# Even layer of a two-layer encoder trunk: the plan that orders its instructions knows three forms of TensorE products, and its ranks are searched anew

## The chip, the cores and the metric

The kernel runs on one core of a Trainium2 chip. The metric is device time in microseconds, the median of several executions. The engines named here are TensorE (PE, with its weight loads PEld), VectorE (DVE), ScalarE (ACT), GpSimd (POOL) and SyncE (SP), which issues the DMAs. Each engine works through its own instructions in the order in which the program gives them, and semaphores hold an instruction back until its inputs are there.

## What is computed

The trunk has two residual layers over 512 tokens of width 1024. Each has a mixer, a layer norm, a convolutional FFN and a second norm. The change touches the mixer of layer 0 alone:

```python
def attn_s5_mixer(x, w_in, sink, a_re, a_im, log_dt, b_re, b_im, c_re, c_im, d_skip, w_glu, w_out):
    z = x @ w_in
    q, k, v, u = jnp.split(z, [ATTN_WIDTH, ATTN_WIDTH + KV_WIDTH, ATTN_WIDTH + 2 * KV_WIDTH], axis=-1)
    y_attn = windowed_gqa(q, k, v, sink)          # 8 heads of 64, window of 128 keys each way
    y_s5 = s5_mixer(u, a_re, a_im, log_dt, b_re, b_im, c_re, c_im, d_skip, w_glu)
    y = jnp.concatenate([y_attn, y_s5], axis=-1)
    return y @ w_out
```

The attention has eight heads and a softmax over up to 384 keys for each block of 128 queries. The S5 part is a bidirectional diagonal complex state-space layer over 32 groups of 16 channels with 64 states each, followed by a GELU and a gate (GLU).

## The kernel before

Every large product is done in three parts of reduced precision: each operand is split into a high part and a low part of type fp32r (`xh`, `xl`, `wh`, `wl`), and `mm3` (line 533) multiplies high by high, high by low and low by high into one PSUM bank. A unit of weights is 512 KB: SP loads it into a staging tile `st` (two of them), ACT casts it to `wh`, and DVE, or POOL for the later units, subtracts to get `wl` (`load_unit`, line 494). `proj_T` (line 539) makes one projection of 128 columns from one unit: 24 products of 512 columns.

The even layer is not issued as it is written. Its methods record steps in a `Plan` (line 200): units 0 to 3 give the S5 inputs (`e_u`), units 4 and 5 give k and v (`e_kv`), units 6 to 9 give q (`e_q`); then come the scores and softmax of each head (`att_scores`), the transposed probabilities times v (`att_out`), and for the S5 part a set-up of narrow steps of 32 columns on DVE (`s_small`, `s_phase`), and for each of four blocks of eight groups the input products (`s_in`), the rotation and the scan on DVE (`s_rot`), tables (`s_out_tables`), the short-range kernel (`s_lags`, with a round trip through DRAM) and the output products (`s_y`, with a second round trip). Three of the four token tiles of the first half of the output projection (`out0` to `out2`) are recorded too; they fill PE where it would wait. Behind the plan GLU (`s_glu`, line 1207) and the rest of the output projection follow, issued in the order in which they are written.

Products come in three shapes of stationary tile. The projections, and the transposes (a product with the identity, `ident`), load a full tile of 128 by 128. The S5 products and the probabilities times v are plain fp32 and use tiles of 128 by 64, one half of the array's columns; each of them stands as two records in the trace. The scores contract over 64 rows: tiles of 64 by 128.

`Plan.order` (line 324) is a list scheduler. It keeps a clock for each engine, knows a cost for every step (`cost`, line 288) and a hop time between engines (`HOP`). Among the steps that can start within 0.06 us of the earliest it takes the one of highest rank:

```python
            s.prio = t + max((steps[u].prio + self.hop(s, steps[u]) for u in s.users), default=0.0)
            s.rank = s.prio + BIAS.get(s.part, 0.0)
```

The rank is the longest weighted path to the end (weights of the engines in `WEIGHT`) plus a number for the step's part, from the table `BIAS`. All engines' instructions, SP's DMAs among them, are issued in the order that results. All instructions of the plan carry line 436, in which they are issued.

Of the kernel before, what the change touches and what calls it, by code (L numbers as in the profile page):

```python
# [45 lines left out]
for _h in range(2, 8):  # L46
    ODD_UNITS += [(c, _h) for c in "qko"]
    if _h % 2 == 1 and _h < 7:
# [11 lines left out]
BIAS = {"act0": 6194, "act1": 110, "act2": 2791, "act3": -1269, "att0": 3695, "att1": 1849, "att2": 2975,  # L60
# [14 lines left out]

WEIGHT = dict(tensor=1.0844148001145095, vector=3.5473736157196103, scalar=0.1530721205110878, gpsimd=0.02, sync=0.09043312895279432)
# [111 lines left out]
class Step:  # L188
    __slots__ = ("eng", "name", "args", "kw", "deps", "users", "cost", "size", "table", "port", "first", "claims", "roots", "prio", "rank", "part", "end", "left", "at")
# [10 lines left out]
class Plan:  # L200
# [4 lines left out]
    HOP = dict(tensor=0.26, vector=0.16, scalar=0.2, gpsimd=0.16, sync=0.1)  # L205
# [30 lines left out]
    def record(self, eng, name, args, kw):  # L236
# [31 lines left out]
        s.port = self.port(s)  # L268
        s.users, s.end, s.at = [], None, None
# [18 lines left out]
    def cost(s):  # L288
        free = lambda v: math.prod(v.shape[1:])
        kw = s.kw  # L290
        if s.eng == "tensor":
            if s.name == "transpose":
                return 2 * free(s.args[1]) / 2400.0
            n = free(kw["rhs"])
            if kw["rhs"].f32r:
                return n / 2400.0 + 0.0133
            n = 4 * max(n, kw["lhsT"].shape[1]) / 2400.0

            return 0.04 if s.args[0].shape[0] == 64 and s.args[0].box[0][0] == 64 else n
# [5 lines left out]
        if s.eng == "scalar":  # L305
            if s.name == "activation":
                s.table = {AF.Exp: 0, AF.Gelu_apprx_tanh: 1, AF.Tanh: 1}.get(kw["func"])
            return 0.085 + 0.00083 * n + 0.09 * sum(not isinstance(kw.get(k, 0.0), float) for k in ("scale", "bias")) + 0.09 * ("accum_out" in kw)
# [15 lines left out]
    def order(self):  # L324
# [8 lines left out]
        table = None  # L333
# [1434 lines left out]
```

## Time and profile before

| | |
|---|---|
| median of 3 runs | 1302.25 us (1301.97 to 1305.85) |
| profiled execution | 1303.45 us, of which the span of instructions is 1301.3 us |
| TensorE busy | 1264.2 us (97%), 6938 products |
| VectorE busy | 717.4 us (55%) |
| ScalarE busy | 547.7 us (42%) |
| GpSimd busy | 138.6 us (11%) |
| planned part | from the start to 230.0 us, when the first product of GLU (line 535) stands on PE |

A busy share says how long an engine had something in work, not how fast it went: records of PE overlap, and their distance from start to start is what one costs. A stretch of the table by window gives the busy time of each engine in it, so that one sees which engine is full there. The chain of waits goes back from the last instruction to what released it, and shows long pieces of one engine where nothing else is waited for.

### The profile page before, as it was taken

How to read it: one execution, taken by the hardware profiler on the slowest of the kernel's cores; microseconds unless marked ns; L12 is line 12 of the kernel's file. 1: busy time of each engine (PE TensorE's matmuls, PEld its weight loads, DVE VectorE, ACT ScalarE, POOL GpSimd, SP SyncE). 2: the span in 40 equal slices, each digit the busy share in tenths (PEclk: the TensorE clock that was granted, in tenths of full speed). 3: DMA queues.
4: the chain of work that ended last, by engine and by line, in shares of the span. 5: the costliest groups of instructions: out<-in, count | busy, mean ns of one | idle time of the engine just before them, and what ended most of it. 6: DMA issues, size and time to landing. Idle time of an engine off the chain costs nothing.

```text
span 1301.3 us, 17757 instructions
## 1 busy us (share of the span) xinstructions
PE 1264.2 (97%) x6938; PEld 1054.9 (81%) x6938; DVE 717.4 (55%) x1402; ACT 547.7 (42%) x919; POOL 138.6 (11%) x139
## 2 busy tenths in 40 slices
PE   3999999999999999999999999999999999999997
PEld 2787777788888888888889898988888888888886
DVE  9887675576442354433674646374865432544415
ACT  4457576344332143332346646472453321433301
POOL 2100322000000000000004444420000000000000
PEclk9999999999999999999999999999999999999999
DMA  5542323534332243323123223223343322433301
GB/s 178 164 127 55 97 90 98 194 98 136 107 93 89 60 140 99 96 93 105 34 91 105 81 82 97 82 65 116 128 144 101 96 87 75 129 97 98 97 33 64
DMA packets 54627, 130.86 MB, mean 101 GB/s; under 512 B 13616, under 2 KB 22144, under 8 KB 53904
## 3 DMA queue, kind: packets, MB, share of 16 engines
q1 hardware_dynamic: 54544, 129.73, 32.3%
q8 instruction: 54, 0.88, 0.3%
q14 instruction: 29, 0.24, 0.1%
HBM read 124.99 MB, written 4.72 MB: 100 GB/s over the span
## 4 chain that ended last, share of the span: by engine, by line
PE 88%; DVE 7%; ACT 2%; issue 1%; DMA 1%; POOL 0%; DVEq 0%; POOLq 0%; ACTq 0%
PE b L559 20%; PE b L536 17%; PE b L535 17%; PE b L537 17%; PE b L436 12%; PE b L1540 1%; PE b L1542 1%; DMA st<-w_dram 1%; DVE x L601 1%; DVE x L579 1%; DVE wl L519 1%; DVE C L436 0%; DVE t L436 0%; ACT wh L518 0%; PE b L1572 0%
## 5 line engine op out<-in xcount | busy, mean ns | idle before, releaser
L536 PE MATMUL b<-xl,wh 128*128 128x512 f32 (+1 forms) x944 | 357.1, 379 | 1.7 <-DVE xl L616 1.7
L535 PE MATMUL b<-xh,wh 128*128 128x512 f32 (+1 forms) x944 | 357.5, 380 | 1.0 <-ACT xh L615 1.0
L537 PE MATMUL b<-xh,wl 128*128 128x512 f32 (+1 forms) x944 | 356.8, 378 | 0.0
L518 ACT CAST wh<-st 128x1024 fp32r<-128x1024 f32 x175 | 183.5, 1051 | 398.2 <-DMA st<-w_dram 144.6
L519 DVE TENSOR_TENSOR wl<-st,wh 128x1024 fp32r<-128x1024 f32 x153 | 186.9, 1224 | 290.4 <-ACT wh L518 286.6
L536 PEld LDWEIGHTS b<-xl,wh 128*128 128x128 f32 x944 | 177.6, 188 | 35.0 <-DVE xl L616 2.4
L535 PEld LDWEIGHTS b<-xh,wh 128*128 128x128 f32 x944 | 177.1, 188 | 34.4 <-ACT xh L615 1.9
L537 PEld LDWEIGHTS b<-xh,wl 128*128 128x128 f32 x944 | 177.6, 188 | 33.2
L559 PE MATMUL b<-wh,hh 128*128 128x512 f32 x352 | 109.2, 389 | 0.0
L559 PE MATMUL b<-wh,hl 128*128 128x512 f32 x352 | 109.2, 389 | 0.0
L559 PE MATMUL b<-wl,hh 128*128 128x512 f32 x352 | 109.1, 389 | 0.0
L598 POOL TENSOR_TENSOR lnrs<-lnsq,mhalf 128x1 f32<-128x1 f32 x16 | 10.5, 657 | 822.2 <-DVE lnsq L597 822.2
L559 PEld LDWEIGHTS b<-wh,hl 128*128 128x128 f32 x352 | 66.1, 188 | 13.7
L559 PEld LDWEIGHTS b<-wl,hh 128*128 128x128 f32 x352 | 66.1, 188 | 13.7
L559 PEld LDWEIGHTS b<-wh,hh 128*128 128x128 f32 x352 | 66.0, 188 | 13.7
L722 DVE TENSOR_TENSOR c<-c,b 128x512 f32<-128x512 f32 x44 | 30.2, 687 | 64.6 <-PE b L537 61.0
L721 ACT ACTIVATE c<-c 128x512 f32<-128x512 f32 x44 | 27.8, 632 | 80.8 <-DVE c L720 80.8
L519 POOL TENSOR_TENSOR wl<-st,wh 128x1024 fp32r<-128x1024 f32 x22 | 52.5, 2390 | 55.6 <-ACT wh L518 55.6
L579 DVE SCALAR_TENSOR_TENSOR x<-x,b 128x512 f32<-128x512 f32 x48 | 31.3, 684 | 43.9 <-PE b L559 40.5
L436 PE MATMUL b<-xh,wh 128*128 128x512 f32 x80 | 33.7, 423 | 11.1 <-ACT wh L436 10.7
L595 ACT ACTIVATE lnjk<-x,lnmu 128x1024 f32<-128x1024 f32 x16 | 18.4, 1152 | 51.4 <-DVE lnmu L594 51.4
L436 PE MATMUL b<-xh,wl 128*128 128x512 f32 x80 | 33.0, 415 | 6.1 <-DVE wl L436 6.1
(332 smaller groups left out, 1924.3 us busy)
## 6 DMA issues: line engine op xcount, KB each, us to landing
st<-w_dram SPq DMA_DIRECT2D x192, 512.0 KB, 3.6
tb<-s5bT_dram SPq DMA_DIRECT2D x16, 256.0 KB, 3.2
lngb<-ln_dram SPq DMA_DIRECT2D x4, 1024.0 KB, 4.8
nb<-DN SPq DMA_DIRECT2D x16, 256.0 KB, 3.6
t<-xT_dram SPq DMA_DIRECT2D x8, 256.0 KB, 7.2
Tj<-DK SPq DMA_DIRECT2D x32, 64.0 KB, 2.3
x<-x_dram SPq DMA_DIRECT2D x1, 2048.0 KB
out_dram<-x SPq DMA_DIRECT2D x8, 256.0 KB, 2.0
```

The source lines that it names most:

```text
L436: getattr(getattr(nc, s.eng), s.name)(*real(s.args), **real(s.kw))
L518: nc.scalar.copy(out=h, in_=x)
L519: eng.tensor_tensor(out=l, in0=x, in1=h.bitcast(F32), op=ALU.subtract)
L535: mm(ps, lhsT=lh, rhs=rh, start=first, stop=False)
L536: mm(ps, lhsT=lh, rhs=rl, start=False, stop=False)
L537: mm(ps, lhsT=ll, rhs=rh, start=False, stop=last)
L559: mm(acc[h], lhsT=hx[:, tok], rhs=wx[:, 512 * h:512 * h + 512], start=a, stop=b)
L579: self.nc.vector.scalar_tensor_tensor(out=xr, in0=xr, scalar=scale, in1=acc[h], op0=ALU.mult, op1=ALU.add, **kw)
L595: nc.scalar.activation(out=jk, in_=x, func=AF.Square, bias=mu, accum_out=sq)
L601: v.scalar_tensor_tensor(out=x[:, c], in0=y[:, c], scalar=rs, in1=b[:, c], op0=ALU.mult, op1=ALU.add)
L721: nc.scalar.activation(out=c, in_=c, func=AF.Gelu_apprx_tanh)
L722: nc.vector.tensor_tensor(out=c, in0=c, in1=pg, op=ALU.mult)
```

## The change

The tables of numbers are replaced, and the planner's rules are changed. It now gives each product on TensorE a form: T for a transpose, R for a product of fp32r (projections and scores alike), F for plain fp32. When a step of PE is taken whose form is another than the last one's, its start is put later by a time from the table `TURN`; and among the candidates a step that keeps the form gets a bonus, `WEIGHT["form"]`, of 20892 on its rank, against biases of up to some 35000. Several costs are set anew (transposes, fp32r and fp32 products, ScalarE's steps with strided input), and one hop. Line numbers in the planned part move by ten (436 becomes 446). Nothing else is changed: the steps, the engines that do them and the buffers are the same.

```diff
-BIAS = {"act0": 6194, "act1": 110, "act2": 2791, "act3": -1269, "att0": 3695, "att1": 1849, "att2": 2975,
+BIAS = {"act0": -2767, "act1": -12777, "act2": -151, "act3": 6961, "att0": 15813, "att1": -1391, "att2": 21019,
...
-WEIGHT = dict(tensor=1.0844148001145095, vector=3.5473736157196103, scalar=0.1530721205110878, gpsimd=0.02, sync=0.09043312895279432)
+WEIGHT = dict(tensor=0.049344435550977735, vector=0.09687933056372891, scalar=858.7347894980174, gpsimd=0.08499304979878007, sync=115.14517424905796, form=20892.369629590066)
...
-    HOP = dict(tensor=0.26, vector=0.16, scalar=0.2, gpsimd=0.16, sync=0.1)
+    HOP = dict(tensor=0.22, vector=0.16, scalar=0.2, gpsimd=0.16, sync=0.1)
+
+    TURN = {"FR": 0.22, "FT": 0.18, "RF": 0.15, "RT": 0.05, "TF": 0.145, "TR": 0.105}
...
+        s.form = None
+        if eng == "tensor":
+            s.form = "T" if name == "transpose" else "R" if kw["rhs"].f32r else "F"
...
             if s.name == "transpose":
-                return 2 * free(s.args[1]) / 2400.0
+                return 0.118
             n = free(kw["rhs"])
             if kw["rhs"].f32r:
-                return n / 2400.0 + 0.0133
-            n = 4 * max(n, kw["lhsT"].shape[1]) / 2400.0
-
-            return 0.04 if s.args[0].shape[0] == 64 and s.args[0].box[0][0] == 64 else n
+                return n / 2400.0 + 0.02
+            return (0.18 if s.args[0].shape[0] == 64 else 0.213) * max(n, kw["lhsT"].shape[1]) / 128
...
-            return 0.085 + 0.00083 * n + 0.09 * sum(not isinstance(kw.get(k, 0.0), float) for k in ("scale", "bias")) + 0.09 * ("accum_out" in kw)
+            if kw["in_"].root.kind not in BANKS and kw["in_"].ap.ap[-1][0] > 1:
+                return 0.06 + 0.00183 * n
+            return 0.1 + 0.00083 * n + 0.09 * sum(not isinstance(kw.get(k, 0.0), float) for k in ("scale", "bias")) + 0.09 * ("accum_out" in kw)
...
-            start, i, take = max(best, key=lambda b: (steps[b[1]].rank, -b[1]))
+            stay = lambda s: WEIGHT["form"] if s.form is not None and s.form == form else 0.0
+            start, i, take = max(best, key=lambda b: (steps[b[1]].rank + stay(steps[b[1]]), -b[1]))
             s = steps[i]
+            if s.form is not None:
+                start = max(start, clock["tensor"] + self.TURN.get(str(form) + s.form, 0.0))
+                form = s.form
```

What this does to the order is seen at three places. In each row stands the line, the operation, the tile written, the tiles read and the shape of the result.

On TensorE, in the middle of the plan (before: a piece of the fourth q projection, `xh` and `xl` times `wh` and `wl`, about 163 us into the span; `ident,s` and `ident,zx` are transposes of probabilities and of S5 tables, `pT,t` probabilities times v), there stands before:

```order
L436 MATMUL b_1690<-xh_82,wl_984 128x512
L436 MATMUL b_1880<-ident_72,s_1749 128x128 x3
L436 MATMUL b_1690<-xh_82,wh_937 128x512
L436 MATMUL b_1690<-xl_83,wh_937 128x512
L436 MATMUL b_1891<-pT_1872,t_892 64x128 x2
L436 MATMUL b_1690<-xh_82,wl_984 128x512
L436 MATMUL b_1901<-ident_72,zx_1709 128x128
L436 MATMUL b_1891<-pT_1893,t_892 64x128 x3
L436 MATMUL b_1901<-ident_72,zx_1709 128x128 x3
L436 MATMUL b_1690<-xh_82,wh_937 128x512
```

On TensorE after, where the probabilities of the same head are at work (`t,t` are scores of the next one):

```order
L446 MATMUL b_1740<-ident_72,s_1422 128x128 x3
L446 MATMUL b_1751<-ident_72,zx_1432 128x128 x4
L446 MATMUL b_1762<-pT_1726,t_648 64x128 x2
L446 MATMUL b_1771<-t_496,t_1133 128x384
L446 MATMUL b_1771<-t_505,t_1133 128x384
L446 MATMUL b_1771<-t_496,t_1142 128x384
L446 MATMUL b_1777<-t_496,t_1133 128x256
L446 MATMUL b_1777<-t_505,t_1133 128x256
L446 MATMUL b_1777<-t_496,t_1142 128x256
L446 MATMUL b_1787<-ident_72,s_1502 128x128 x3
L446 MATMUL b_1791<-ident_72,zx_1769 128x128 x4
```

The wide products of the projection have gone from between the others to a row of their own, and transposes of both kinds stand together.

On VectorE, around its first low part of x (`xl`), with steps of the S5 set-up (`T`, `th`, `al`, `ns`, `ea`, `eb`, `ec`), before, some 80 rows into its order:

```order
L436 TENSOR_TENSOR th_277<-ee_235,ed_248 128x32
L436 TENSOR_TENSOR T_97<-t_53_239,t_54_242 128x64
L436 TENSOR_TENSOR al_281<-fh_269,ed_248 128x32
L436 TENSOR_TENSOR t_53_239<-T_97 128x128
L436 TENSOR_TENSOR t_54_242<-T_97 128x128
L436 TENSOR_SCALAR ns_286<-pv_73 128x8
L436 TENSOR_TENSOR T_97<-t_53_239,t_54_242 128x128
L436 TENSOR_TENSOR xl_83<-t_111,xh_82 128x512
```

On VectorE after, at the head of its order:

```order
L446 TENSOR_TENSOR xl_83<-t_100,xh_82 128x512
L446 TENSOR_TENSOR wl_150<-st_102,wh_146 128x1024
L446 TENSOR_SCALAR ea_157<-KS_113 128x32
L446 TENSOR_SCALAR eb_160<-ea_157 128x32
L446 TENSOR_SCALAR eb_160<-eb_160 128x32
L446 SCALAR_TENSOR_TENSOR ec_164<-eb_160,ea_157 128x32
L446 TENSOR_SCALAR ee_166<-eb_160 128x32
L446 TENSOR_TENSOR wl_168<-st_109,wh_153 128x1024
```

The low parts have moved ahead of the set-up, whose input `KS` also comes later: SP loads it first before, and after x's first two pieces, two weight units and a bias tile now.

On VectorE after, at the low part of weight unit 5 (`wl_523`, the v projection; `C` are S5 tables, `t_499` and `t_505` k):

```order
L446 TENSOR_TENSOR C_444<-bc_138,b_406 128x512
L446 TENSOR_TENSOR ea_468<-fa_488 128x32
L446 TENSOR_TENSOR t_499<-b_415,t_490 64x512
L446 TENSOR_TENSOR t_505<-b_415,t_496 64x512
L446 CAST t_499<-t_499 64x512
L446 CAST t_505<-t_505 64x512
L446 TENSOR_TENSOR eb_472<-fb_485 128x32
L446 SCALAR_TENSOR_TENSOR p_89_519<-fa_488,fb_485 128x32
L446 TENSOR_TENSOR p_89_519<-ea_468,eb_472 128x32
L446 TENSOR_TENSOR wl_523<-st_326,wh_429 128x1024
```

On TensorE after, the products that read it:

```order
L446 MATMUL b_299<-xh_82,wh_280 128x512
L446 MATMUL b_299<-xl_83,wh_280 128x512
L446 MATMUL b_299<-xh_82,wl_301 128x512
L446 MATMUL b_529<-ident_72,zx_512 128x128 x4
L446 MATMUL b_474<-xh_82,wl_523 128x512
L446 MATMUL b_474<-xh_82,wh_429 128x512
```

Ahead of the four transposes here stand 122 wide products and nothing else on PE; before, half-width products came in after 91 wide ones and eight transposes.

## Rows read from the trace of the kernel before

**Rows 1.** The page, busy time: engine, us, share of span, instructions.

```profile
PE 1264.2 (97%) x6938; PEld 1054.9 (81%) x6938; DVE 717.4 (55%) x1402; ACT 547.7 (42%) x919; POOL 138.6 (11%) x139
```

**Rows 2.** By window: length, busy PE, PEld, DVE, ACT, POOL; granted clock, DMA, GB/s.

```profile
0.00:28.00 28.00, 8.22 (x18) 5.31 (x19) 24.89 (x110) 12.62 (x21) 9.05 (x16) 1.00 0.64 207
28.00:47.30 19.30, 18.86 (x83) 14.72 (x82) 19.17 (x80) 6.63 (x12) 0.00 (x0) 1.00 0.44 133
47.30:103.60 56.30, 55.29 (x567) 45.72 (x566) 48.82 (x106) 29.80 (x49) 8.00 (x15) 1.00 0.45 132
103.60:138.00 34.40, 32.07 (x273) 24.24 (x273) 26.00 (x63) 23.62 (x54) 4.63 (x13) 0.95 0.23 58
138.00:174.00 36.00, 35.88 (x319) 26.52 (x317) 23.97 (x57) 25.25 (x55) 10.57 (x17) 1.00 0.30 89
174.00:199.00 25.00, 25.00 (x265) 20.54 (x265) 16.12 (x50) 19.76 (x46) 6.26 (x10) 1.00 0.31 93
199.00:212.40 13.40, 13.28 (x71) 9.12 (x70) 13.36 (x18) 8.41 (x19) 6.72 (x3) 1.00 0.44 126
212.40:230.00 17.60, 17.60 (x158) 14.37 (x157) 5.39 (x7) 11.79 (x17) 0.00 (x0) 1.00 0.29 74
sum 230.00, PE 206.20 PEld 160.54 DVE 177.73 ACT 137.89 POOL 45.24; mean PE 25.77 PEld 20.07 DVE 22.22 ACT 17.24 POOL 5.66
```

**Rows 3.** Chain of waits: start us, us, what; first wide product of GLU last.

```profile
170.72 40.19 PE b L436 x349
...
230.13 0.23 PE b L535
```

**Rows 4.** Timeline of PE: start us, us, line, out<-in, stationary tile, moving tile, records.

```profile
162.65 0.39 PE L436 MATMUL b<-xh,wl 128*128 128x512 f32 x1
162.88 0.49 PE L436 MATMUL b<-ident,s 128*128 128x128 f32 x3
163.12 0.48 PE L436 MATMUL b<-xh,wh 128*128 128x512 f32 x1
163.44 0.40 PE L436 MATMUL b<-xl,wh 128*128 128x512 f32 x1
163.77 0.65 PE L436 MATMUL b<-pT,t 128*64 128x128 f32 x4
164.35 0.50 PE L436 MATMUL b<-xh,wl 128*128 128x512 f32 x1
164.69 0.27 PE L436 MATMUL b<-ident,zx 128*128 128x128 f32 x1
164.89 0.87 PE L436 MATMUL b<-pT,t 128*64 128x128 f32 x6
165.69 0.55 PE L436 MATMUL b<-ident,zx 128*128 128x128 f32 x3
165.99 0.48 PE L436 MATMUL b<-xh,wh 128*128 128x512 f32 x1
```

**Rows 5.** Timeline of PE, early: in brackets the idle time before and its end.

```profile
19.01 0.80 PE L436 MATMUL b<-xh,wl 128*128 128x512 f32 x1 [5.91 <-DVE wl L436]
...
47.00 0.39 PE L436 MATMUL b<-xl,wh 128*128 128x512 f32 x1
47.34 0.44 PE L436 MATMUL b<-C,B 128*64 128x128 f32 x4
47.71 0.50 PE L436 MATMUL b<-xh,wl 128*128 128x512 f32 x1
48.04 0.40 PE L436 MATMUL b<-xh,wh 128*128 128x512 f32 x1
```

**Rows 6.** Timelines of ACT (the last high part of x) and DVE, early.

```profile
18.04 0.60 ACT L436 CAST xh<-t 128x512 fp32r<-128x512 f32 x1
...
23.57 1.22 DVE L436 TENSOR_TENSOR wl<-st,wh 128x1024 fp32r<-128x1024 f32 x1
24.71 3.67 DVE L436 TENSOR_TENSOR C<-bc,b 128x512 f32<-128x512 f32 x6
```

More of the change, by code (lines that the diff above doesn't have):

```diff
@@ L188 @@
 class Step:
-    __slots__ = ("eng", "name", "args", "kw", "deps", "users", "cost", "size", "table", "port", "first", "claims", "roots", "prio", "rank", "part", "end", "left", "at")
+    __slots__ = ("eng", "name", "args", "kw", "deps", "users", "cost", "size", "table", "port", "form", "first", "claims", "roots", "prio", "rank", "part", "end", "left", "at")
 class PlanEngine:
@@ L332, in order @@
         warm, window, busy = False, 0, 0.0
-        table = None
+        table = form = None
         slots, nxt = {}, {}
```

29 rows, old and new, of the table BIAS are left out of this document.

## Prediction, made before the changed kernel was run

> **What bounds the kernel now.** I read the page first: TensorE (PE) is busy for 97% of the span, VectorE (DVE) for 55% [rows 1]. The change touches only the planned even layer, so the next view is the table by stretch of its first 230 us [rows 2]. Columns two and four carry the argument. From 28 us on PE is busy in nearly every microsecond, while DVE is busy for 19.17 of 19.30 us, then 48.82 of 56.30, and later for 16.12 of 25.00: it is the full engine first and has room later. In the chain of waits the long pieces are TensorE's own: one of 349 products takes 40.19 us with no wait inside [rows 3]. So in the planned stage a microsecond saved on PE counts, as long as DVE delivers.
>
> PE's busy time is no measure of its work, since records overlap; the timeline with its start times is [rows 4]. In an unbroken row a wide product (f32r, 512 columns) takes 0.23 us [rows 3]. Three transposes set between two of them cost only themselves: from 162.65 to 163.44 pass 0.79 us, which is two wide products and 0.33, or 0.11 a transpose. The half-width fp32 records `pT,t` are dearer. Four of them pass in 0.58 us (163.77 to 164.35), six in 0.80 (164.89 to 165.69): 0.11 a record, and 0.14 on top. The wide product before the four takes 0.33 instead of 0.23, the one behind them 0.34. That is 0.35 us for one excursion from the full array (128*128 in the rows) to half of it (128*64) and back: 0.175 a change. Over the whole piece from 163.44 to 165.99 the parts (two wide products, ten records, four transposes) make 2.00 of 2.55 us; the rest over four changes is 0.14 each. At 47.00 to 48.04 [rows 5] the wide product before the four `C,B` records takes 0.34, the one behind them 0.33, and the four nothing on top: 0.21 us for two changes, 0.105 each. So the ends are 0.105 and 0.175; I take 0.15, since most changes that go are around `pT`, `U` and score products, as in the first place.
>
> **The change, part by part.**
>
> *Fewer changes of shape on TensorE.* The instructions are the same in number and kind (592 fp32, 408 f32r, 148 transposes); only their order differs. I counted in both orders where the shape of the stationary tile changes (full 128*128; half width 128*64; the score products, 64*128): 173 times before, 69 after, 104 fewer. At 0.15 us this is **-15.6 us**, between -10.9 (0.105) and -18.2 (0.175), all on the engine that sets the stage's pace. The planner itself counts differently: forms F, R and T, with score products among R and transposes apart; in its count 191 turns become 76, 115 fewer.
>
> The Trainium skill ("TensorEngine Tiling (Array Packing)", Key Properties) says that changing the tiling mode, not just the tile, drains the engine. The rows bear it out: transposes among wide products are free, half-width ones are not. By that rule 104 counts and not 115, which at 0.15 would be 17.3 us.
>
> *An earlier start.* Before, DVE works through the S5 set-up first; PE waits for the low part of the first weights until 19.01 us [rows 5]. After, the low parts `xl` and `wl` stand at the head of DVE's order, and PE's order opens with 122 wide products in a row. How far it gets is set by DVE. The last low part of x needs the last high part: 18.04 + 0.60 = 18.6 us before [rows 6], and after too, since the same transfers stand ahead of it in SP's queue. DVE has done 7.3 us of work by then (four `xl`, at 0.6 as any step of 512 columns, two `wl` at 1.14, both [rows 6], and 15 narrow steps of the set-up, some 2.6). What must be done up to `wl` of weight unit 5 (the v projection): the 24.89 us that DVE did in the first 28 us [rows 2], plus three `xl` (1.8), four `wl` at 1.14 (4.6), four copies of k at 0.6 (2.4) and about 1.1 of small steps: 34.8 us. So this `wl` is ready at 18.6 + 0.6 + (34.8 - 7.3) = 46.7 us. PE waits for it with 122 wide products and 4 transposes done; before, at 47.34, it had done 91 and 8 [rows 5]. Lead: 31 x 0.23 - 4 x 0.11 = 6.7, and 0.6 of time: **-7.3 us**. If DVE reaches it 7 us later, for instance because s5s now lands behind x0, w0, bias and w1 and the set-up waits for it, the lead is nothing; if it comes when the wide products are there, it is about 9.
>
> *Where TensorE alone would end.* Before, PE needs 182.7 us from 47.3 to the end of the plan at 230.0. Less 6.7 and 15.6 this is 160.4, from 46.7: 207.1 us.
>
> *What DVE then allows.* DVE's own work is the same, but less of it is done when PE is further. Of its 177.73 us [rows 2], 34.8 are done at 46.7 us and 2.7 (four steps of 512 columns, as `xl`) lie behind the last scan block (rot3: `rb`, `S`); 140.2 remain. Behind rot3 PE has its tail: before, 17.60 us from 212.40 to 230.00 [rows 2]; after, 27 instead of 36 wide products stand there, so 15.6. With DVE never waiting: 46.7 + 140.2 + 15.6 = 202.5. DVE's best long stretches are 99% (28.00:47.30) and 87% (47.30:103.60). Midway, 93%, gives 150.8 and an end at 213.1. That is later than PE's own 207.1, so DVE's pace is the likelier limit: **+6.0 us** against TensorE alone. The ends are 0 and 16.3 (87%: 223.4).
>
> *The new rules of the planner* (costs, hop, turn times) cost nothing on the chip: they act through the order only. SP's order moves too: s5s later, `bias` between the two DK writes of lags 2 and 3 (SP waits there until the four score tiles of a head are read). Their consumers, y2 and y3, stand over 15 us of PE work later, which hides this; without that cover each costs a few microseconds, and it is inside the ends above.
>
> Behind the plan the order is written by hand and unchanged: GLU and output projection move with the end of the plan. The last S5 block goes through DRAM once more before GLU, with 27 wide products and pv7 behind it on PE; nine fewer than before, which leaves that round trip less cover but, by my sum, enough.
>
> Sum against the profiled execution, 1303.45 us (median of the three runs 1302.25, 1.2 less): -15.6 - 7.3 + 6.0 = -16.9 (end of the plan at 213.1 instead of 230.0): **1286.5, rounded 1286**.
>
> **The rivals.**
>
> (a) *TensorE alone sets the end.* DVE keeps over 97%, and waits vanish on both: end 202 to 207, time 1276 to 1281. For it: DVE's 99% early, when its inputs lay ready. Against it: DVE waits in order for scores that PE makes, and PE for DVE.
>
> (b) *DVE at 87%*, its pace in 47 to 104 us before: end 223.4, -6.6 us, 1297. For it: the same mix of steps, in-order waits. Against it: it was then fed by a PE that lost time on changes.
>
> (c) *The changes were hidden anyway*, so that the grouping buys nothing: then only the lead of 7.3 is left, 1296; with a slow DVE as well, no change. Against it: [rows 4] show the loss between products that wait for nothing.
>
> (d) *Slower: DVE's set-up comes too late and DVE is fed as before.* From 47.3 to 212.4 it was busy for 128.3 of 165.1 us, 78%. At that pace 140.2 us take 180, the plan ends at 242.7 and the time is 1316. It decides from 83.6% down: (230.0 - 46.7 - 15.6) = 167.7 us are there for 140.2. Against it: in these stretches PE was full (25.00 of 25.00), so DVE's idleness followed from PE's.
>
> **How the numbers follow.** Forecast (DVE between 90 and 96%, 1281 to 1291): 0.50. (a) 0.20. (b), with times from 1291 to 1298: 0.12. (c) 0.05 at 1296, and a further 0.06 with a slow DVE, within 0.3%. (d) 0.07. A measurement of this kernel can tell about 0.3% (3.9 us) from no change; so faster 0.50 + 0.20 + 0.12 + 0.05 = 0.87, same 0.06, slower 0.07. The range must leave out no more than 0.2: from 1276 (a TensorE without any wait) to 1298 it leaves out some 0.05 below and 0.13 above.
>
> **What would show it.** In the trace after, starts on PE: an early stretch of 122 wide products up to about 46 us with a wait for `wl` in it; far fewer places with 128*64 rows between 128*128 rows, each still dearer by 0.1 to 0.17 us; GLU's first product at 207 to 218 us; DVE busy for over 90% between 47 us and the last scan. I am wrong if PE shows more idle time than some 10 us after 47 us, if a change of shape costs nothing when no wait is near, or if GLU starts with a wait for the last S5 block.

## The result

The changed kernel takes 1283.97 us (median of four runs, 1282.96 to 1285.5), the kernel before 1302.67 beside it: a ratio of 0.9853, 95% interval 0.9833 to 0.9872, so faster by 1.5%. Forecast were 1286 us, range 1276 to 1298. The profiled run took 1284.29 us. Its page, busy time as in [rows 1]:

```profile
PE 1239.7 (97%) x6938; PEld 1044.2 (81%) x6938; DVE 715.7 (56%) x1402; ACT 547.1 (43%) x919; POOL 135.8 (11%) x139
```

The share of TensorE says nothing: 97% before and after. The table by stretch, to be held against [rows 2], is cut at four places of the prediction: x's last low part ready, `wl` of unit 5 ready, the end of the last scan block, GLU's first product.

```profile
0.00:17.40 17.40, 8.95 (x30) 6.42 (x31) 10.49 (x24) 8.32 (x11) 6.86 (x15) 1.00 0.93 296
17.40:42.60 25.20, 22.59 (x98) 17.47 (x96) 23.55 (x108) 14.43 (x25) 0.61 (x5) 1.00 0.44 140
42.60:193.90 151.30, 137.11 (x1470) 115.17 (x1471) 137.17 (x352) 104.81 (x217) 35.40 (x53) 0.97 0.39 113
193.90:209.90 16.00, 12.75 (x148) 10.47 (x146) 4.38 (x6) 9.93 (x15) 0.00 (x0) 1.00 0.13 35
```

Two things are to be seen. The plan ends at 209.9 us instead of 230.1 [rows 3], 20.2 earlier (the span is 19.1 shorter; the 1.1 us lie between 610 and 1035 us, in code that no part of the change touches). And from 42.6 us on it is VectorE (third pair) that is as full as TensorE: 137.17 of 151.30 us, against 128.3 of 165.1 before (the prediction's sum from [rows 2]). TensorE, which stood still for 3.2 us behind 47 us before, now waits for 17.3 there, in 23 waits. The table of waits names the largest (engine, tile and line, for whom: us in all, times, longest):

```profile
PE b L446 <- ACT pT L446: 7.1, 8, 2.2
PE b L446 <- ACT KS L446: 2.2, 3, 1.0
PE b L446 <- DVE m L446: 2.0, 1, 2.0
```

The start of TensorE, as [rows 5]: 122 wide products and four transposes have started by 41.3 us, where before 92 and 8 had by 47.34 (the count of 91 made ahead of the run is one short). Then comes the forecast wait for `wl`, of 1.03 us.

```profile
39.64 0.39 PE L446 MATMUL b<-xh,wl 128*128 128x512 f32 x1
40.93 0.66 PE L446 MATMUL b<-ident,zx 128*128 128x128 f32 x4 [0.91 <-ACT zx L446]
42.62 0.50 PE L446 MATMUL b<-xh,wl 128*128 128x512 f32 x1 [1.03 <-DVE wl L446]
```

TensorE was also slower at the start of the kernel before. Up to 28.2 us its wide products stand 0.43 us apart, as they do in stretches with a granted clock of 0.50 (0.427 us in e2 below), and 0.23 us from there on:

```profile
27.34 0.63 PE L436 MATMUL b<-xl,wh 128*128 128x512 f32 x1
27.76 0.60 PE L436 MATMUL b<-xh,wl 128*128 128x512 f32 x1
28.44 0.40 PE L436 MATMUL b<-xh,wl 128*128 128x512 f32 x1
28.67 0.39 PE L436 MATMUL b<-xh,wh 128*128 128x512 f32 x1
```

In the changed kernel they stand 0.23 us apart from 11.3 us on. The trace's record of the granted clock begins only at these points, 28.2 and 11.1 us, and the tables print 1.00 for what lies ahead of them.

GLU's first product follows the plan's last two (a row that starts at 209.45) without a wait, at 209.90.

**What the prediction had not seen** stands in the rows of half-width products. Their outputs go to partitions 0 to 63 or to 64 to 127, that is, their stationary tiles stand on one half of the array's columns or on the other. Before, at 192.54 us, four records of `So,C` (two products of one half) take 0.28 or 0.24 us:

```profile
192.54 0.45 PE L436 MATMUL b<-So,C 128*64 128x64 f32 x4
192.82 0.28 PE L436 MATMUL b<-U,T 128*64 128x64 f32 x2
192.94 0.40 PE L436 MATMUL b<-So,C 128*64 128x64 f32 x4
193.18 0.28 PE L436 MATMUL b<-U,T 128*64 128x64 f32 x2
```

In the changed kernel the same products take turns between the halves, and eight records pass in the same 0.24 us (183.39 to 183.63), four of `U,T` in 0.11 where before there were two:

```profile
183.39 0.40 PE L446 MATMUL b<-So,C 128*64 128x64 f32 x8
183.63 0.29 PE L446 MATMUL b<-U,T 128*64 128x64 f32 x4
183.74 0.40 PE L446 MATMUL b<-So,C 128*64 128x64 f32 x8
183.98 0.29 PE L446 MATMUL b<-U,T 128*64 128x64 f32 x4
```

A 64-column fp32 product thus costs 0.117 us behind one on its own half, and 0.058 behind one on the other half: the two run at the same time. The Trainium skill says so ("TensorEngine Tiling (Array Packing)", Key Properties: "Tiles operate independently: Different tiles can execute LdWeights and Matmul in parallel"); the rows agree. The prediction drew on the sentence that stands above it, on the drain, and not on this one. It is the half that counts and not the PSUM bank that they write: on the same half, products into different banks stand 0.116 us apart (median of 144 in the kernel before), and on different halves products into the same bank 0.058 (216 in e12 below). In the plan's order two half-width products in a row stood on different halves 132 times of 512 before, and 383 times of 565 after.

**An account of TensorE.** I took the start times of all 1148 products of the plan, in both traces. A stretch of one shape is charged what its products take in an unbroken row (wide 0.227, half-width as above); what is on top of that up to 0.3 us is put down to the change of shape behind it, and more to a wait; stretches that touch half clock stand apart. Behind 28 us, from before to after: wide products and transposes 57.5 to 47.7 us (the lead: they are done earlier), half-width products 74.7 to 60.1, changes of shape 23.4 to 10.5, waits 2.8 to 15.4, half clock 2.2 to 7.9. That is -9.8 - 14.6 - 12.9 + 12.6 + 5.7 = -19.0 of the 20.1 us. (The last row of wide products, 34 before and 27 after, is not in the account; it is 1.6 us more of the lead.) Three gains, of which one was not forecast, and two losses, of which the forecast knew one in another form.

### The profile page after: what moved, and what is told of

Read it like the earlier page. It is cut to its first block, busy times and chain, and to the rows that moved or that the text cites. A ratio compares the mean times of both kernels' runs of the same rounds, so it can differ in the third digit from the quotient of the medians.

```text
span 1282.2 us, 17748 instructions
## 1 busy us (share of the span) xinstructions
PE 1239.7 (97%) x6938; PEld 1044.2 (81%) x6938; DVE 715.7 (56%) x1402; ACT 547.1 (43%) x919; POOL 135.8 (11%) x139
## 4 chain that ended last, share of the span: by engine, by line
PE 82%; DVE 9%; ACT 3%; DMA 2%; issue 2%; POOL 1%; SPq 0%; DVEq 0%; POOLq 0%; ACTq 0%
PE b L569 21%; PE b L546 18%; PE b L545 18%; PE b L547 18%; PE b L446 5%; DMA st<-w_dram 2%; PE b L1550 1%; PE b L1552 1%; DVE t L446 1%; DVE x L611 1%; DVE x L589 1%; DVE C L446 1%; DVE wl L529 1%; SPq L446 0%; DVE c L446 0%
## 5 line engine op out<-in xcount | busy, mean ns | idle before, releaser
L545 PE MATMUL b<-xh,wh 128*128 128x512 f32 (+1 forms) x944 | 357.7, 380 | 1.0 <-ACT xh L625 1.0
L545 PEld LDWEIGHTS b<-xh,wh 128*128 128x128 f32 x944 | 177.1, 188 | 34.4 <-ACT xh L625 1.9
L608 POOL TENSOR_TENSOR lnrs<-lnsq,mhalf 128x1 f32<-128x1 f32 x16 | 10.5, 657 | 840.5 <-DVE lnsq L607 840.5
L569 PEld LDWEIGHTS b<-wh,hl 128*128 128x128 f32 x352 | 66.1, 188 | 13.7
L569 PEld LDWEIGHTS b<-wl,hh 128*128 128x128 f32 x352 | 66.1, 188 | 13.7
L569 PEld LDWEIGHTS b<-wh,hh 128*128 128x128 f32 x352 | 66.0, 188 | 13.6
L545 PE MATMUL b<-wh,xh 128*128 128x256 f32 (+1 forms) x128 | 37.0, 289 | 0.3 <-ACT xh L625 0.3
```

Source lines behind the costliest of these rows:

```text
L545: mm(ps, lhsT=lh, rhs=rh, start=first, stop=False)
L569: mm(acc[h], lhsT=hx[:, tok], rhs=wx[:, 512 * h:512 * h + 512], start=a, stop=b)
```

## Experiments

All plans have the same 1148 products. "Turns" are pairs of half-width products in a row that stand on different halves. "Waits" is the sum of TensorE's table of waits from 47 us to the plan's end; "half clock" is the time between 12 and 238 us in which the granted clock was 0.5, summed from a table by 2 us. The slow start is not in it, since the record of the clock begins behind it: at 28 to 31 us in the kernel before, e1, e4, e5 and e12, at 11 to 16 us in the others.

| kernel | changes of shape | turns | waits us | half clock us | last product of the plan at | time us | ratio to before, 95% |
|---|---|---|---|---|---|---|---|
| before | 173 | 132 of 512 | 3.2 | 3.4 | 229.7 | 1302.7 | |
| changed | 69 | 383 of 565 | 17.3 | 10.2 | 209.7 | 1284.0 | 0.9853 (0.9833 to 0.9872) |
| e1 regroup | 95 | 149 of 551 | 5.4 | 3.4 | 216.8 | 1289.8 | 0.9878 (0.9856 to 0.9900) |
| e2 split | 173 | 363 of 524 | 10.1 | 27.3 | 226.3 | 1299.2 | 0.9954 (0.9935 to 0.9973) |
| e3 no bonus | 144 | 388 of 525 | 21.4 | 20.5 | 233.6 | 1319.2 | 1.0108 (1.0084 to 1.0132) |
| e5 bonus alone | 94 | 125 of 552 | 15.3 | 20.4 | 237.9 | 1314.1 | 1.0070 (1.0048 to 1.0092) |
| e4 late start | 69 | 383 of 565 | 22.6 | 13.6 | 227.6 | 1302.4 | 0.9985 (0.9969 to 1.0001) |
| e6 early start | 167 | 135 of 515 | 19.0 | 20.5 | 237.5 | 1312.8 | 1.0078 (1.0055 to 1.0101) |
| e7 VectorE relieved | 69 | 383 of 565 | 11.6 | 6.8 | 201.6 | 1276.3 | 0.9795 (0.9773 to 0.9817) |
| e8 TensorE relieved | 69 | 383 of 565 | 22.8 | 30.7 | 213.7 | 1286.6 | 0.9873 (0.9851 to 0.9895) |
| e9 queues | 69 | 383 of 565 | 15.0 | 10.2 | 208.4 | 1280.6 | 0.9828 (0.9808 to 0.9848) |
| e10 search | 82 | 287 of 556 | 16.5 | 27.3 | 214.7 | 1288.6 | 0.9886 (0.9864 to 0.9907) |
| e11 search with lock | 77 | 274 of 557 | 13.7 | 6.8 | 205.7 | 1278.7 | 0.9808 (0.9782 to 0.9835) |
| e12 sides | 95 | 436 of 551 | 7.7 | 6.8 | 211.7 | 1284.6 | 0.9858 (0.9828 to 0.9889) |

Where only the order is other, the kernel has this edit and a list of step numbers:

```diff
-        done = self.order()
+        self.order()
+        done = [self.steps[i] for i in ORDER]
```

### What a change of shape costs, and that it counts

**e1.** The order of before, on TensorE alone with stretches exchanged. For instance (TensorE, at 47 us in [rows 5]; out<-in, columns):

```diff
 MATMUL b<-xl,wh 128x512
-MATMUL b<-C,B 64x128 x2
-MATMUL b<-xh,wl 128x512
-MATMUL b<-xh,wh 128x512
-MATMUL b<-C,B 64x128 x6
-MATMUL b<-xl,wh 128x512
...
 MATMUL b<-xl,wh 128x512
+MATMUL b<-C,B 64x128 x16
```

> The kernel before, with its own ranks, its own start and its own order on every engine but TensorE; there, neighbouring stretches of products are exchanged (none over 8 us, and only where the trace of before shows that the inputs of what comes earlier were there and that the reader of what comes later was not yet waiting), so that the tile shape changes 95 times instead of 173. Theory 1 (each change costs TensorE some 0.15 us, and TensorE's time counts): 78 x 0.15 = 11.7 us less, 1291; 1295 if a third of it goes into waits of its own. Theory 2 (the grouping buys nothing, the gain of the changed kernel is its earlier start): 1302, no change.

1289.77 us, 15.0 less than before beside it (1304.74). The plan's last product starts 12.9 us earlier, which is 0.165 a change for 78 changes, while TensorE's waits grew by 2.2 us only. Its largest waits, before and in e1:

```profile
PE b L436 <- ACT s L436: 1.5, 1, 1.5
PE b L541 <- ACT So L541: 1.8, 2, 1.0
```

So the grouping pays by itself, with before's start and ranks: theory 1. In the account of e1 the places of change fall from 23.4 to 10.1 us, and the turns hardly move (half-width products 74.7 to 73.4). The median of what a change adds in the kernel before is 0.15 us behind full-array stretches, 0.14 behind half-width ones, 0.19 behind score products (57, 78 and 33 stretches).

**e2.** The changed kernel, cut up again on TensorE until the shape changes 173 times:

```diff
-MATMUL b<-U,t 64x64 x2
-MATMUL b<-ident,s 128x128 x4
+MATMUL b<-U,t 64x64
+MATMUL b<-ident,s 128x128
+MATMUL b<-U,t 64x64
+MATMUL b<-ident,s 128x128 x3
```

> The changed kernel, with its start and the order of every other engine as they are; on TensorE, behind 28 us, stretches of two shapes that stand side by side are cut into two pieces each and interleaved, by the same conditions on inputs and readers, until the shape changes 173 times as before the change, instead of 69. Theory 1 (0.15 us a change on TensorE): 104 x 0.15 = 15.6 us more, 1299.6; 1294 if a third of it falls into waits that are there anyway. Theory 2 (the changes are hidden): 1284 to 1286.

1299.2, as theory 1 has it, but not as clean as it looks. The account gives 12.9 us more at changes of shape; 7.0 us of waits go, since work now fills them; and 7.8 us come from TensorE's clock. In the table by stretch the granted clock (third number from the end) is 0.52 for 17.5 us and 0.66 for 10, where the changed kernel had 1.00 but for 10 us in all:

```profile
142.00:152.00 10.00, 9.67 (x88) 7.34 (x87) 6.81 (x19) 8.62 (x16) 4.72 (x2) 0.66 0.64 171
152.00:170.50 18.50, 17.84 (x229) 13.83 (x225) 15.74 (x30) 14.22 (x27) 9.72 (x11) 1.00 0.53 157
170.50:188.00 17.50, 16.16 (x58) 10.46 (x59) 10.46 (x24) 8.93 (x22) 3.77 (x7) 0.52 0.45 135
```

Half-width products add 1.3. So of e2's 15 us 12.9 are the price of 104 changes (0.12 each), and the other three terms nearly cancel; that the time meets theory 1 is more than the theory deserves.

### Ranks and bonus: neither works alone

**e3** and **e5.** The bonus off with the new ranks; the bonus alone on the old ones.

```diff
-WEIGHT = dict(tensor=0.049344435550977735, vector=0.09687933056372891, scalar=858.7347894980174, gpsimd=0.08499304979878007, sync=115.14517424905796, form=20892.369629590066)
+WEIGHT = dict(tensor=0.049344435550977735, vector=0.09687933056372891, scalar=858.7347894980174, gpsimd=0.08499304979878007, sync=115.14517424905796, form=0.0)
```

> The changed kernel with its new ranks and new costs, but the bonus for the form that stands on TensorE set to 0: 144 changes of shape instead of 69. Theory 1: 75 x 0.15 = 11.3 us more, 1295, if the ranks alone set the waits. Theory 2 (the new ranks bring the gain by themselves, the bonus little): 1284 to 1287. Theory 3 (ranks and bonus were searched together, and neither works alone): over 1300, with waits on TensorE of over 20 us behind 47 us.

```diff
-            start, i, take = max(best, key=lambda b: (steps[b[1]].rank, -b[1]))
+            stay = lambda s: 5000.0 if s.form is not None and s.form == form else 0.0
+            start, i, take = max(best, key=lambda b: (steps[b[1]].rank + stay(steps[b[1]]), -b[1]))
             s = steps[i]
+            if s.form is not None:
+                form = s.form
```

> The kernel before with its ranks and costs, and the bonus for the form that stands on TensorE as the only addition (5000, within the spread of its ranks): 94 changes of shape instead of 173, as many as in the regrouped kernel. Theory 1 (the number of changes decides): 79 x 0.15 = 11.9 less, 1291, like the regrouped kernel. Theory 3 (fewer changes by a rule that doesn't look at who waits only turn the gain into waits): 1300 to 1310, with over 10 us more of waits on TensorE than the regrouped kernel has.

1319.2 and 1314.1: both slower than before, so theory 1 falls for both. Theory 3 holds for e3. For e5 it holds in kind: the time is above its range (1300 to 1310), and the waits are 9.9 us more than in e1 where over 10 were expected; the bonus was tried at one value, 5000. e5 is the sharper of the two: it has as many changes of shape as e1 (94 and 95) and stands 24 us above it. TensorE's largest waits, in e3 and then in e5:

```profile
PE b L446 <- DVE t L446: 7.2, 10, 1.5
PE b L446 <- ACT So L446: 4.8, 2, 3.2
```

```profile
PE b L442 <- DVE t L442: 7.2, 6, 2.5
PE b L442 <- ACT pT L442: 2.4, 7, 0.6
PE b L442 <- DVE ra L442: 1.9, 1, 1.9
```

Their sums are 21.4 and 15.3 us, with half clock for 20 us in both. In e3 the last S5 block comes too late as well: GLU (L545) waits 5.0 us for it, and 9.4 of its 33 us more of span lie behind the plan. The turns tell where the side-by-side products come from: e3 has them (388 of 525), e5 has not (125 of 552). So they come with the new costs and ranks, and not with the bonus; which of those two does it was not tried.

### The start is no sum of its own

**e4** and **e6.** The first 360 steps of before, then the changed order; the first 339 of the changed kernel, then before's order (both by a list, as above).

> The first 360 steps of the plan of before (up to its 100th product on TensorE, at 47 us), and behind them all others in the order of the changed kernel: the lead is taken away, the 69 changes of shape stay. Theory 1 (the lead is worth what TensorE has done more by then: 126 products at 41.3 us instead of 99 at 47.3, some 11 us): 1284 + 11 = 1295. Rival (the lead melts in waits that come later anyway): 1284 to 1288.

> The first 339 steps of the plan of the changed kernel (up to its 128th product on TensorE, at 43 us), and behind them all others in the order of before: the lead without the grouping, 167 changes of shape. Theory 1 (the lead is a sum of its own): 1302.5 - 11 = 1291. Rival (the lead is paid by VectorE's set-up, which is 58 steps behind in this start, and an order that isn't searched to that waits for it): 1302 or more.

Both numbers of theory 1 fall. Without the lead the grouped order loses 18 us and not 11: 1302.4, no faster than before. TensorE waits 4.5 us at one place for `wl` and 22.6 in all. With the lead, before's order is 10 us slower than before: the set-up on VectorE, put off, comes back in one piece when that order asks for it. TensorE's timeline in e6:

```profile
58.00 0.44 PE L541 MATMUL b<-C,B 128*64 128x128 f32 x1 [13.54 <-DVE C L541]
```

So the early start is worth what the order behind it makes of it: from -10 (e6) to +18 us (e4 against the changed kernel). Neither order was searched as a whole, so these are the prices of two splices; what the best order with either start would take was not tried.

### Who sets the plan's end now

**e7** and **e8** take nearly as much work from VectorE and from TensorE, with every instruction in its place. In e7, 24 steps of 0.68 us take 0.22, which is 11.1 us less by their records (12.8 was expected); in e8, 118 products take 0.118 us instead of 0.227, 12.9 us less (17 of them stand ahead of 46 us, from 35.7 on).

```diff
+                if s.eng == "vector" and s.name == "tensor_tensor" and math.prod(s.kw["out"].shape) == 65536 and s.kw["out"].root is s.kw["in0"].root:
+                    cut = (lambda x: x[:, 0:64]) if len(s.kw["out"].shape) == 2 else (lambda x: x[:, :, 0:2, :])
+                    kw.update({k: cut(kw[k]) for k in ("out", "in0", "in1")})
```

> The changed kernel with its order as it is; the 24 in-place steps of 512 columns on VectorE (S, ra and C, 0.68 us each) work on an eighth of their columns, so that part of the scan sums and tables is left out: some 12.8 us less work on VectorE between 46 and 194 us. Theory A (VectorE's pace sets the plan's end, as predicted): the end comes by most of that earlier, 1272 to 1276. Theory B (TensorE's own work and waits for single steps that stand in line on other engines set it): 0 to 3 us less, 1281 to 1284.

```diff
+                if s.form == "R" and not kw["start"] and not kw["stop"] and tuple(kw["rhs"].shape) == (128, 512) and tuple(args[0].shape) == (128, 512):
+                    n += 1
+                    if n > 90 and n % 5 < 3:
+                        args, kw = (args[0][:, 0:256],), {**kw, "rhs": kw["rhs"][:, 0:256]}
```

> The changed kernel with its order as it is; behind 46 us 118 wide products of the plan work on 256 of their 512 columns, so that half of those sums is left out: 118 x 0.11 = 12.9 us less work on TensorE, as much as the other kernel takes from VectorE. Theory A (VectorE's pace sets the end): 0 to 3 us less, 1281 to 1284. Theory B: more than half of it, 1271 to 1277.

Less work on VectorE brings the plan's end forward by 8.1 us and the time to 1276.3; less work on TensorE brings nothing, 1286.6. That is theory A, with two reservations. In e7 the half clock is 3.4 us shorter as well, worth up to 1.7 of the 8.1 us, and up to its last scan block (187.0 us) VectorE is busy for 86% only (123.56 of 144.40 us):

```profile
42.60:187.00 144.40, 134.16 (x1463) 113.78 (x1463) 123.56 (x352) 105.23 (x219) 34.80 (x53) 0.98 0.41 118
```

In e8 TensorE's clock was halved for 30.7 us instead of 10.2, which at half speed takes back up to 10 us of the 12.9. The longest such stretch in e8's table:

```profile
62.00:78.00 16.00, 13.55 (x107) 11.68 (x107) 12.49 (x35) 4.71 (x15) 2.87 (x3) 0.57 0.30 87
```

So e8 shows that TensorE with less to do waits more (22.8 us) and runs slower, not that its work is free. That VectorE's work counts rests on e7; that it alone sets the end is not shown.

**e9.** Are the 17 us of waits a matter of places in line?

```diff
+COPY pT<-b 128x256
+COPY pT<-b 128x256
 CAST wh<-st 128x1024
-COPY pT<-b 128x256
-COPY pT<-b 128x256
```

> The changed kernel; on TensorE, POOL and SP every instruction stands where it stood. On ScalarE seven steps that copy transposed scores (pT), for which TensorE waited 0.9 to 2.5 us at 104, 137, 152 and 197 us while ScalarE did something else or waited for a weight tile, go ahead of what stood before them; on VectorE the score step that TensorE waited for at 164.8 us goes ahead of the KS step that took 2.35 us there. Theory B (these waits are places in line on other engines, and TensorE, which they hold up, sets the end): 5 to 7 us of waits go, and with them the 6.8 us of half clock behind 164 us, worth up to 3: 1275 to 1279. Theory A (VectorE's pace sets the end, and TensorE's waits only show it): 0 to 2 us less, 1282 to 1284, the waits come again at other places.

1280.6, 0.25% below the changed kernel by the ratios, whose intervals overlap; the plan's last product stands 1.3 us earlier. (The profiled run is the slowest of five, 1283.65, with 3.4 us of half clock at 911 us, far behind the plan.) The longest wait is now 1.5 us, where there were two of over 2 us, but the waits still sum to 15.0 us instead of 17.3, in 26 places instead of 23, and the stretch of half clock behind 164 us now stands at 140. The time lies between what the two theories forecast (1275 to 1279 and 1282 to 1284); that the waits came back elsewhere speaks for theory A.

### Can the order do better?

> The same instructions as the changed kernel, but the order on all engines searched further, step by step, from the changed kernel's, with durations, transfer times, 0.13 to 0.17 us per change of shape and the lock between VectorE and POOL as the traces of the two kernels show them; 82 changes of shape. If waits on single steps are what is left (TensorE waits for 17 us behind 47 us in the changed kernel), most of them can go: plan's end some 6 to 9 us earlier, 1274 to 1278. If VectorE's pace is a limit that no order moves (93% busy up to 194 us): 1281 to 1285.

> Again the same instructions, in an order searched step by step from the changed kernel's on all engines, but with two things that the searched kernel before it (82 changes of shape, 1288.6) left out: a VectorE step with both inputs in SBUF waits until a POOL step that runs at that moment has ended (there, four steps of 0.2 us took 2.3 us beside a POOL step), and each transfer and step may be late by a random amount, so that no place hangs on a single one. 77 changes of shape. If the lock and such waits are what the first search lost: 1272 to 1278, with under 10 us of waits on TensorE behind 47 us and half its clock for less than 10 us. If the order has no more to give, because VectorE's pace and TensorE's work meet: 1281 to 1288.

e10 missed: 1288.6. Two things stand in its trace that can have taken the gain: half clock (27.3 us), and the lock shown in the last section. By its own expectation the lock had been counted; that of e11 says that a form of it had been left out. e11, which counts that form and lets steps be late at random, takes 1278.7: just above what was expected if lock and waits were the loss, and below both kernels. Its half clock is 6.8 us, as expected; its waits (13.7 us) did not fall below 10. Which of the two additions made it faster is not shown, since its order is another one throughout.

**e12.** e1 with the halves taking turns, all else in its place. For instance:

```diff
-MATMUL b<-C,B 64x128 x16
-MATMUL b<-U,t 64x64
-MATMUL b<-U,t 64x64
-MATMUL b<-nU,t 64x64
...
+MATMUL b<-C,B 64x128 x10
+MATMUL b<-U,t 64x64 x2
+MATMUL b<-U,t 64x64 x2
+MATMUL b<-nU,t 64x64 x2
+MATMUL b<-U,t 64x64 x2
+MATMUL b<-C,B 64x128 x6
```

> The regrouped kernel (the kernel before with 95 changes of shape, all ranks, the start and every other engine's order as before), with one thing more: inside its stretches of half-width fp32 products on TensorE, which stay where they are, products that write partitions 0 to 63 and products that write partitions 64 to 127 take turns. Two half-width products in a row stand on different halves 436 times instead of 149 (of 551). Theory 1 (products on the two halves of the array run at the same time, so that a 64-column product behind one on the other half costs 0.058 us and behind one on its own half 0.117): 287 x 0.058 = 16.6 us less than the regrouped kernel, 1273; 1276 to 1280 if other engines can't follow. Theory 2 (the order inside such a stretch is free, and what the changed kernel gained beyond its start came from fewer changes of shape alone): 1288 to 1291, as the regrouped kernel.

The rows show the mechanism by itself: products that passed two by two in e1 (first fence) pass four by four in e12 in the same time.

```profile
180.99 0.40 PE L541 MATMUL b<-So,C 128*64 128x64 f32 x4
181.23 0.28 PE L541 MATMUL b<-U,T 128*64 128x64 f32 x2
181.34 0.40 PE L541 MATMUL b<-So,C 128*64 128x64 f32 x4
```

```profile
178.33 0.40 PE L541 MATMUL b<-So,C 128*64 128x64 f32 x8
178.56 0.29 PE L541 MATMUL b<-U,T 128*64 128x64 f32 x4
178.68 0.40 PE L541 MATMUL b<-So,C 128*64 128x64 f32 x8
```

So the order inside such a stretch is not free, as theory 2 has it, and 1284.6 is outside its range; but it is outside that of theory 1 too (1273, or 1276 to 1280). The plan's end comes 5.1 us earlier than in e1. Of the 17.6 us that the half-width products save by the account, 3.9 come back as waits, 2.1 as half clock and 6.0 at the changes of shape (0.18 a change, 0.11 in e1; why, the runs don't show). By the time alone e12 and e1 are hardly apart, their intervals overlap, and up to 2.2 of the 5.1 us may have another cause: a step `S<-S,ra` of e1 at 197.72 us takes 2.85 us beside a step of POOL (the lock of the last section), and in e12 all eight take 0.7 or less. It is the rows that show the mechanism. e12 also shows that the early start was not needed for this time: with TensorE's order alone changed it is as fast as the changed kernel (1284.6 and 1284.0).

## Why the prediction held, point by point

**The bound before** was read rightly: with only TensorE's order changed (e1), the plan's end comes 12.9 us earlier (15.0 by the times).

**Fewer changes of shape, -15.6.** Right in mechanism and nearly in size: 0.15 us was taken, the medians are 0.14 to 0.19, e1 gives 0.165 all in, the account of the changed kernel 12.9 us. Rival (c), that the changes were hidden, is refuted by e1.

**An earlier start, -7.3.** The step "DVE has done 7.3 us of work by then" failed. When the last low part of x was ready, at 17.4 us and not at 19.2, VectorE had done 10.49 us. To the end of `wl` it needed 34.0 us (10.49 + 23.55; forecast 34.8) and stood idle for 1.65. So `wl` came at 42.6 and not at 46.7. The 122 wide products and four transposes were right. With them, and with the 92 wide products that stood there before, the lead is 6.0 us of time and 6.4 of work (30 wide products more, four transposes less), less some 1.2 us of waiting: 11.2 instead of 7.3. And e4 and e6 show that such a lead is no term that one may add by itself.

**What VectorE then allows, +6.0.** The three pieces of the sum were 46.7 + 150.8 + 15.6; they came as 42.6 + 151.3 + 16.0. VectorE ran at 90.7% (137.17 of 151.30) where 93% was taken, with 137.2 us left instead of 140.2, of which 4.3 are not work but two steps that POOL locked out (last section). That it is VectorE's pace that counts is what e7 shows, with the reservations above. Rivals (b) at 87% and (d) below 83.6% didn't occur, nor did (a): TensorE doesn't set the end alone.

**Where TensorE alone would end, 207.1.** This was wrong, in two halves that hid each other. TensorE lost 17.3 us by waits behind 47 us, so that the sign against me ("more idle time than some 10 us after 47 us") was met: without the 14.1 us more of waits it would have ended near 196 by this sum. It could have, because its half-width products run side by side (14.6 us less in the account), which the sentence "cost nothing on the chip: they act through the order only" passes over. [rows 5] had a trace of it: the two `C,B` products at 47.34 us stand on different halves and take 0.37 us with their change of shape, where two of 128 columns on one half take 0.44 without (0.218 each, the median). The prediction read this as a cheap change of shape, 0.105. The old planner's cost rule, which the diff takes away, counts 0.04 us for a product whose output starts at partition 64; that was the place to ask why. That the two halves nearly cancel (14.6 and 14.1 us) is luck. The forecast did not rest on it, since by its sum VectorE's pace gave the later end, and that sum came within 3.2 us.

**The planner's new rules.** Taken by themselves as free, which they are; but the expectation behind it, that the number of changes decides, is refuted by e5. In this kernel the grouping rule paid only with ranks that were searched with it.

## What to carry to other kernels

Before adding up what an order saves on the busiest engine, work out when the second engine would finish at the paces it has shown so far; here that sum held (213.1 forecast, 209.9 measured) although two mechanisms on the first engine were missing from it. On TensorE, fp32 products with 64-column stationary tiles should take turns between the two halves of the array (0.058 us each here, instead of 0.117), and stand together rather than between full-width ones (0.14 to 0.19 us a change here). A rule in a scheduler and the ranks that were searched with it are one change: tried apart, each made this kernel slower.

## What the hardware showed beside that

**A VectorE step can be locked out by POOL.** In the changed kernel a step on 16 x 64 elements takes 0.216 us in the median of eight, and once 2.345. The view of the tile `KS` (durations in ns, least, median and largest):

```profile
L446 DVE TENSOR_TENSOR KS<-KS,k x8: 206/216/2345, 70.2 to 171.5; 16x64 f32<-16x64 f32 x8
```

On VectorE's timeline of the changed kernel it is this row:

```profile
161.96 2.35 DVE L446 TENSOR_TENSOR KS<-KS,k 16x64 f32<-16x64 f32 x1
```

It began while POOL made a `wl`, and ended with it (164.23 and 164.31 us), as POOL's timeline has it:

```profile
161.87 2.36 POOL L446 TENSOR_TENSOR wl<-st,wh 128x1024 fp32r<-128x1024 f32 x1 [5.36 <-ACT wh L446]
```

The Trainium skill ("SBUF — State Buffer", "SBUF: two separate sides") calls the port pair of VectorE and GpSimd an exclusive lock that is held for the whole instruction, when the VectorE step has two SBUF inputs and the GpSimd step reads SBUF, as here; the rows agree. Such a step counts as busy, so that VectorE's busy share hides it; here it cost TensorE the wait of 2.0 us for `m`. A second one, `c<-bc,th` at 132.87 us, takes 2.45 us instead of 0.28 beside a POOL step that runs to 135.17. The kernel before has it in its last scan block, where [rows 2] show VectorE full (13.36 of 13.40 us): the first of two steps takes 2.77 us, with a median of 0.68, beside a step of POOL from 208.72 to 211.25.

```profile
209.03 3.37 DVE L436 TENSOR_TENSOR S<-S,ra 128x512 f32<-128x512 f32 x2
```

In e10 three steps that elsewhere take 0.2 to 0.3 us took 2.3 us in this way (not four, as the expectation of e11 has it); its timeline of VectorE:

```profile
128.14 2.34 DVE L551 TENSOR_TENSOR e<-E,ph 128x32 f32<-128x32 f32 x1
...
132.44 2.32 DVE L551 TENSOR_TENSOR KS<-KS,DG 80x64 f32<-80x64 f32 x1
...
140.55 2.35 DVE L551 TENSOR_TENSOR B<-c 64x128 f32<-64x128 f32 x1
```

**A wait on TensorE can cost twice.** Behind the same wait the granted clock stands at 0.50, the lower of its two levels (1.2 GHz), for 6.8 us; in the 7.7 us ahead of that TensorE was busy for 4.71. The table by stretch of the changed kernel, the clock third from the end:

```profile
157.00:164.70 7.70, 4.71 (x62) 3.89 (x58) 6.56 (x12) 6.35 (x14) 2.83 (x4) 1.00 0.21 72
164.70:171.50 6.80, 6.74 (x43) 5.08 (x43) 3.57 (x10) 4.25 (x8) 2.39 (x3) 0.50 0.65 183
171.50:178.00 6.50, 6.50 (x49) 5.14 (x46) 6.17 (x15) 4.95 (x15) 0.11 (x1) 1.00 0.43 137
```

Over the fourteen kernels the time at half clock runs from 3.4 to 30.7 us. It has a part in the results of e2, e3, e5, e6, e8 and e10; the forecast could hardly read it from the kernel before, where it was 3.4 us behind the start.
